# Second feed-forward of an encoder block: sums on VectorE, operands split one at a time, raw weights of the last matrix loaded from ScalarE's queue

## The chip, the cores and the metric

One core of a Trainium2 chip (trn2) runs the whole kernel. The core has a matrix engine (TensorE, PE in the profile), three engines for elementwise work (VectorE, DVE; ScalarE, ACT; GpSimd, POOL), an engine that mostly issues transfers (SyncE, SP), and 16 DMA engines that all queues share. An engine works through its own instructions in order; between engines, instructions wait on semaphores. The metric is device time in microseconds (us) for one execution.

## The reference

One layer of a streaming encoder over 1024 frames and 16 meta tokens, width 1024. The part that matters here is the last step, a SwiGLU feed-forward with 2816 hidden columns:

```python
def rmsnorm(x, g):
    xf = x.astype(jnp.float32)
    y = xf * lax.rsqrt(jnp.mean(xf * xf, axis=-1, keepdims=True) + EPS)
    return (y * g.astype(jnp.float32)).astype(x.dtype)

def swiglu(x, w_gate, w_up, w_down):
    return (jax.nn.silu(x @ w_gate) * (x @ w_up)) @ w_down
...
        h = h + mixed @ w_out[l]

        h = h + 0.5 * swiglu(rmsnorm(h, ffn2_norm[l]), ffn2_w_gate[l], ffn2_w_up[l], ffn2_w_down[l])
    return rmsnorm(h, final_norm)[:, N_META:]
```

Everything is fp32. Ahead of this come a first feed-forward, the attention, the gated linear attention and the merge; the change does not touch them.

## The kernel before

**Precision.** Each fp32 operand x is split in a rounded part hi (a cast on ACT) and a rest lo = x - hi (a subtraction on DVE); `halves` does both and puts hi and lo side by side in one tile. A product of two operands is three matmuls: hi*hi, hi*lo, lo*hi. A matmul is 128x128 weights against 512 columns.

**Seven products.** Data are transposed: 128 rows of features, 512 columns of tokens, so each feature tile has two token halves c = 0, 1. The two large matrices of the second feed-forward use a scheme with seven block products in place of eight (Strassen and Winograd), `PRODUCTS`: for the weights the blocks A11, A12, A22 and the sums S1 to S4, for the data B11, B21, B22 and T1 to T4. The products accumulate in three PSUM banks in the order b, a, b, d, b, d, b, and after a product the bank is read out, before a later product goes on adding to it. `Group.sums` makes S1 to S4 from two raw tiles, `Group.weights(i)` splits the weight operand of product i into a ring of eight tiles (wop), `Group.product` issues the matmuls. The scheduler runs the weights some seven products ahead, as far as the ring allows.

**Stages, in order of time.**

- w_out: for c = 0, 1 and m = 0 to 7 a product of 24 matmuls, the addition to h on DVE, a store to memory (h2_dram), and the sum of squares for the norm (acc). After each c, `scales_total` (a product with ones, tot, then the root, the reciprocal and a diagonal matrix dg) and `scales_spread` (a transpose, rep) turn acc into scales, and `rescale` and `halves` make the operands.
- Hidden tiles f = 0, 1 by ordinary products (`plain`), while T1 to T4 of the data are formed and split (tt).
- gate/up, `gate_up(f)`, f = 2 to 21: seven products of 12 matmuls, 84 in all. The raw tiles of gate and up come over SP's queue. ACT copies the bank after product 0 (L1172, g0), after product 2 (L1179, g1) and after product 3 (L1182, u1); DVE adds after products 1, 4, 5; ACT does the Silu; the two products of gate and up are on POOL (u1, L1189) and DVE. After two f, `middle` makes the seven data operands of the last matrix (B11, B21, T2, T1, T3, B22, T4); `keep` splits each (kh on ACT, kl on DVE) and stores both to memory (mid_dram).
- down: five groups (kg) of four hidden tiles, two halves each, 84 matmuls per half. Data operands (tm) are loaded from mid_dram, 512 KB each, raw weights in four loads of 256 KB per half, and h in tiles, all over SP's queue, in the order of the code. After each half product DVE adds half of the bank to h (L1252). There are two raw tiles, so a raw tile of the half after next waits until the last reader of the one in its place is done: casts, splits and POOL's sums.
- The last two hidden tiles by ordinary products, the final norm and the output.

## Time and profile before

| | |
|---|---|
| median of 3 runs | 2170.28 us (2168.26 to 2174.21) |
| the profiled execution | 2174.23 us |
| its span in the profile | 2172.5 us |
| mean granted TensorE clock | 0.987 |
| busy: TensorE, DVE, ACT, POOL | 2102.6, 1188.9, 707.8, 358.4 us |
| w_out between its column halves | 1387.4 to 1393.7 us |
| gate/up, f = 2 to 21 | 1484.55 to 1921.31 us |
| down | 1921.31 to 2129.26 us |

Times in the trace are from the start of the span. A row of a timeline has its start, its duration, the engine, the line, the operation, output and inputs, shapes, and in brackets the idle time just before it with what released it. Durations of matmuls overlap, since matmuls are pipelined: from start to start an undisturbed one takes less than its own duration. A row of waits has the waiting group, what it waited for, the total, how often, and the longest. A row of groups has the busy time and the mean of one in ns, then the idle time before them.

### The profile page before, as it was taken

The page shows a single profiled execution, that of the slowest core. Times are in us where ns is not written, and L with a number is a line of the kernel's source. Part 1 is how long each engine was busy: PE and PEld are TensorE (multiplying, and loading weights), DVE is VectorE, ACT ScalarE, POOL GpSimd, SP SyncE. Part 2 cuts the span into 40 slices and gives each one's busy share as a digit, 9 for nine tenths or more (in the row PEclk, how much of TensorE's full clock was granted, in tenths as well). Part 3 has the DMA queues.
Part 4 walks back from the last instruction along what each step waited for, and adds up shares of the span by engine and source line. Part 5 has one row for each costly group of instructions (what it writes and reads, how often), then busy time and mean ns, then how long its engine had stood idle before and what let it go on. Part 6 is the DMA issues. An engine that isn't in the chain of part 4 may idle for free.

```text
span 2172.5 us, 28898 instructions
## 1 busy us (share of the span) xinstructions
PE 2102.6 (97%) x11225; PEld 1866.1 (86%) x11225; DVE 1188.9 (55%) x1986; ACT 707.8 (33%) x1333; POOL 358.4 (16%) x320
## 2 busy tenths in 40 slices
PE   9999999999999999999999999998999999998998
PEld 8999999999999998888997788786777777786887
DVE  4644454444544446773534347458666556666776
ACT  6221111211112345663334233334443444322222
POOL 1000000000000260000100000124443435323322
PEclk9999999999999999999999999998999999999999
DMA  4211111111111221226112235533344334498732
GB/s 138 78 50 48 40 59 40 49 49 40 56 42 45 85 65 49 59 68 196 51 40 71 71 102 187 176 103 103 130 141 150 117 126 150 141 358 292 289 107 78
DMA packets 227641, 230.20 MB, mean 106 GB/s; under 512 B 19622, under 2 KB 174368, under 8 KB 227504
## 3 DMA queue, kind: packets, MB, share of 16 engines
q1 hardware_dynamic: 225840, 225.61, 32.1%
q10 hardware_dynamic: 1312, 2.63, 0.3%
q8 instruction: 88, 1.44, 0.3%
q14 instruction: 49, 0.40, 0.1%
q0 software_dynamic: 352, 0.11, 0.0%
HBM read 164.35 MB, written 63.96 MB: 105 GB/s over the span
## 4 chain that ended last, share of the span: by engine, by line
PE 85%; DVE 6%; DMA 4%; issue 2%; ACT 2%; POOL 1%; SPq 0%; DVEq 0%; POOLq 0%; ACTq 0%
PE pj L96 6%; PE pj L98 5%; PE pj L97 5%; PE pd L97 4%; PE pd L96 4%; PE pd L98 4%; PE pg L96 4%; PE pu L96 4%; PE pg L98 4%; PE pb L1112 4%; PE pg L97 4%; PE pu L98 4%; PE pu L97 4%; PE pb L1114 4%; PE pb L1113 4%
## 5 line engine op out<-in xcount | busy, mean ns | idle before, releaser
L204 ACT CAST whi<-raw 128x1024 fp32r<-128x1024 f32 x124 | 129.0, 1049 | 401.3 <-PE pd L97 189.8
L96 PE MATMUL pj<-u2h,whi 128*128 128x512 f32 (+2 forms) x608 | 228.8, 376 | 1.7 <-DVE o L902 1.7
L97 PE MATMUL pj<-u2l,whi 128*128 128x512 f32 (+2 forms) x608 | 223.7, 368 | 0.0
L98 PE MATMUL pj<-u2h,wlo 128*128 128x512 f32 (+2 forms) x608 | 223.7, 368 | 0.0
L96 PE MATMUL pg<-u1h,whi 128*128 128x384 f32 (+1 forms) x528 | 169.7, 321 | 2.0 <-ACT whi L204 2.0
L205 DVE TENSOR_TENSOR wlo<-raw,whi 128x1024 fp32r<-128x1024 f32 x121 | 149.1, 1239 | 40.2 <-ACT whi L204 35.2
L96 PE MATMUL pu<-u1h,whi 128*128 128x384 f32 (+1 forms) x528 | 169.6, 321 | 0.6 <-ACT u1q L181 0.6
L98 PE MATMUL pg<-u1h,wlo 128*128 128x384 f32 (+1 forms) x528 | 169.1, 320 | 0.6 <-DVE wlo L205 0.6
L97 PE MATMUL pg<-u1l,whi 128*128 128x384 f32 (+1 forms) x528 | 169.0, 320 | 0.0
L97 PE MATMUL pd<-ml,whi 128*128 128x384 f32 (+1 forms) x528 | 168.9, 320 | 0.0
L98 PE MATMUL pd<-mh,wlo 128*128 128x384 f32 (+1 forms) x528 | 168.5, 319 | 0.0
L96 PE MATMUL pd<-mh,whi 128*128 128x384 f32 (+1 forms) x528 | 168.5, 319 | 0.0
L98 PE MATMUL pu<-u1h,wlo 128*128 128x384 f32 (+1 forms) x528 | 168.4, 319 | 0.0
L97 PE MATMUL pu<-u1l,whi 128*128 128x384 f32 (+1 forms) x528 | 168.2, 319 | 0.0
L284 DVE SCALAR_TENSOR_TENSOR h<-pd,h 128x384 f32<-128x384 f32 (+1 forms) x240 | 122.8, 518 | 80.0 <-PE pd L98 79.3
L143 POOL TENSOR_TENSOR u2q<-u2q,sq 128x384 f32<-128x384 f32 (+1 forms) x21 | 19.6, 935 | 715.8 <-ACT sq L142 715.8
L1112 PE MATMUL pb<-tt,wop 128*128 128x512 f32 x240 | 99.3, 414 | 35.9 <-ACT g L1172 21.7
L96 PEld LDWEIGHTS pj<-u2h,whi 128*128 128x128 f32 x608 | 114.2, 188 | 20.6 <-issue 2.2
L98 PEld LDWEIGHTS pj<-u2h,wlo 128*128 128x128 f32 x608 | 114.1, 188 | 17.1
L1017 DVE TENSOR_TENSOR wop<-s,wop 128x512 fp32r<-128x512 f32 x120 | 93.6, 790 | 62.6 <-ACT wop L1016 62.2
L97 PEld LDWEIGHTS pj<-u2l,whi 128*128 128x128 f32 x608 | 114.3, 188 | 15.1
L1016 ACT CAST wop<-s 128x512 fp32r<-128x512 f32 x120 | 73.2, 623 | 136.3 <-POOL s L1095 65.5
(378 smaller groups left out, 4985.1 us busy)
## 6 DMA issues: line engine op xcount, KB each, us to landing
tm<-mid_dram SPq DMA_DIRECT2D x70, 512.0 KB, 8.9
raw<-in_ffn_w_gate SPq DMA_DIRECT2D x44, 512.0 KB, 4.0
raw<-in_ffn_w_up SPq DMA_DIRECT2D x44, 512.0 KB, 4.0
mid_dram<-kh SPq DMA_DIRECT2D x70, 256.0 KB, 2.3
mid_dram<-kl SPq DMA_DIRECT2D x70, 256.0 KB, 2.0
raw<-in_w_in SPq DMA_DIRECT2D x30, 512.0 KB, 3.9
raw<-in_ffn_w_down SPq DMA_DIRECT2D x24, 512.0 KB, 3.6
raw<-in_ffn_w_down SPq DMA_DIRECT2D x40, 256.0 KB, 4.8
```

The costliest lines, as they stand in the source:

```text
L96: nc.tensor.matmul(ps, wh[k], xh[k], start=(k == 0), stop=False)
L97: nc.tensor.matmul(ps, wh[k], xl[k], start=False, stop=False)
L98: nc.tensor.matmul(ps, wl[k], xh[k], start=False, stop=(k == n - 1))
L143: nc.gpsimd.tensor_add(a, a, sq[:, 0:n])
L204: nc.scalar.copy(hi[:, 0:cols], raw[:, 0:cols])
L205: (eng or nc.vector).tensor_sub(lo[:, 0:cols], raw[:, 0:cols], hi[:, 0:cols].bitcast(F32))
L284: nc.vector.scalar_tensor_tensor(hm, ps[:, 0:n], 0.5, hm, op0=ALU.mult, op1=ALU.add)
L1016: nc.scalar.copy(x[:, 0:HALF], src)
L1017: nc.vector.tensor_sub(x[:, HALF:], src, x[:, 0:HALF].bitcast(F32))
L1112: nc.tensor.matmul(ps, wh, xh, start=(first and k == 0), stop=False, skip_group_check=True)
L1113: nc.tensor.matmul(ps, wh, xl, start=False, stop=False, skip_group_check=True)
L1114: nc.tensor.matmul(ps, wl, xh, start=False, stop=(k == n - 1), skip_group_check=True)
```

## The change

Four things, in the order of the program:

1. The scales of the first column half of w_out and the rescaling and splitting of its eight tiles move from between the two column halves into the second one: the total behind product m = 0, the transpose behind m = 1, the tiles behind m = 1 to 7.
2. In gate/up the sums S1 to S4, the product for u1 and the differences of the pair move from POOL to DVE, and so do the differences for T1 to T4 ahead of it, where those of T4 are made only as T4 is split. `Group.sums` gets the engine as an argument; in down it stays POOL.
3. What `middle` makes of a pair goes to a list, `pending`, and `pump` takes one operand from it after each product of the following f: its difference, its split, its stores. After the last f the rest is emptied.
4. In down the raw weights are loaded over ACT's queue, issued ahead of product 6 of the half before. The loads of the data operands alternate with those of h, one operand at a time.

A small tile, shift2, is placed ahead of two of the ring's tiles; it only shifts an address.

```diff
@@ -1041,7 +1041,15 @@
             ps = bank("wo")
             cols = slice(c * HALF, (c + 1) * HALF)
             mm(ps, wh, wl, [t[:, cols] for t in mx_[0]], [t[:, cols] for t in mx_[1]])
+            if c == 1 and m == 0:
+                first_dg = scales_total(accs[0])
+            if c == 1 and m == 1:
+                scales_spread(accs[0], first_dg)
             nc.vector.tensor_add(hm, ps, hm)
+            if c == 1 and m >= 1:
+                for k in (range(2) if m == 1 else [m] if m < KT else []):
+                    rescale(k, 0)
+                    tops["B11" if k < 4 else "B21"][k % 4] = halves(operand(t_a, "tb"), ub[0][k])
             nc.sync.dma_start(out=h2_dram[c, m], in_=hm)
             if m == 0:
                 nc.scalar.activation(acc, hm, AF.Square)
@@ -1049,11 +1057,6 @@
                 sq = ttile("sq")
                 nc.scalar.activation(sq, hm, AF.Square)
                 (nc.vector if m >= KT - 2 else nc.gpsimd).tensor_add(acc, acc, sq)
-        if c == 0:
-            scales_spread(acc, scales_total(acc))
-            for m in range(KT):
-                rescale(m, 0)
-                tops["B11" if m < 4 else "B21"][m % 4] = halves(operand(t_a, "tb"), ub[0][m])
     acts.close()
 
     f2 = ctx.enter_context(ExitStack())
@@ -1061,6 +1064,8 @@
     shift = t_b.tile([P, 32], F32, name="shift", bufs=1)
     nc.gpsimd.memset(shift, 0.0)
     w_ext = f2.enter_context(tc.tile_pool(name="wext2", bufs=2))
+    shift2 = w_ext.tile([P, 32], F32, name="shift2", bufs=1)
+    nc.gpsimd.memset(shift2, 0.0)
     s_pool = f2.enter_context(tc.tile_pool(name="sums", bufs=4))
     ring, slot = [w_main] * 6 + [w_ext] * 2, [0]
 
@@ -1087,12 +1092,12 @@
             self.a = {"A11": a1[:, 0:HALF], "A12": a1[:, HALF:], "A21": a2[:, 0:HALF], "A22": a2[:, HALF:]}
             self.banks = {}
 
-        def sums(self):
+        def sums(self, eng):
             a = self.a
             for s, x, y, add in (("S1", "A21", "A22", True), ("S2", "S1", "A11", False),
                                  ("S3", "A11", "A21", False), ("S4", "A12", "S2", False)):
                 a[s] = s_pool.tile([P, HALF], F32, tag="s", name="s")
-                (nc.gpsimd.tensor_add if add else nc.gpsimd.tensor_sub)(a[s], a[x], a[y])
+                (eng.tensor_add if add else eng.tensor_sub)(a[s], a[x], a[y])
 
         def weights(self, i):
             w = ring_tile("wop")
@@ -1121,7 +1126,7 @@
     NAMES = [n for _, _, n in PRODUCTS]
     mid_dram = dram.tile([2 * NG, 7, P, 2 * HALF], F32, name="mid_dram")
     last_dram = dram.tile([LAST, 2, P, 2 * HALF], F32, name="last_dram")
-    pair = []
+    pair, pending = [], []
 
     def keep(dst, src):
         hi, lo = block("kh", F32R), block("kl", F32R)
@@ -1134,7 +1139,7 @@
 
         if f >= NF - LAST:
             for c, x in enumerate((m0, m1)):
-                keep(last_dram[f - (NF - LAST), c], x)
+                pending.append(lambda c=c, x=x: keep(last_dram[f - (NF - LAST), c], x))
             return
         pair.append((m0, m1))
         if f % 2 == 0:
@@ -1143,17 +1148,22 @@
         pair.clear()
         d = mid_dram[f // 2]
         t1, t2 = block("tm"), block("tm")
-        keep(d[NAMES.index("B11")], b11)
-        nc.vector.tensor_sub(t1, b12, b11)
-        nc.gpsimd.tensor_sub(b12, b22, b12)
-        keep(d[NAMES.index("B21")], b21)
-        nc.vector.tensor_sub(t2, b22, t1)
-        keep(d[NAMES.index("T2")], t2)
-        nc.gpsimd.tensor_sub(b21, b21, t2)
-        keep(d[NAMES.index("T1")], t1)
-        keep(d[NAMES.index("T3")], b12)
-        keep(d[NAMES.index("B22")], b22)
-        keep(d[NAMES.index("T4")], b21)
+
+        def work(n, src, sums=()):
+            def go():
+                for x in sums:
+                    nc.vector.tensor_sub(*x)
+                keep(d[NAMES.index(n)], src)
+            return go
+
+        pending.extend([
+            work("B11", b11, [(t1, b12, b11)]), work("B21", b21, [(b12, b22, b12)]),
+            work("T2", t2, [(t2, b22, t1)]), work("T1", t1, [(b21, b21, t2)]),
+            work("T3", b12), work("B22", b22), work("T4", b21)])
+
+    def pump():
+        if pending:
+            pending.pop(0)()
 
     def gate_up(f):
         raws = []
@@ -1170,24 +1180,31 @@
         b = product(0)
         g0 = block("g0")
         nc.scalar.copy(g0, b)
+        pump()
         a = product(1)
-        g.sums()
         nc.vector.tensor_add(g0, a, g0)
+        g.sums(nc.vector)
         nc.scalar.activation(g0, g0, AF.Silu)
+        pump()
         product(2)
         g1 = block("g1")
         nc.scalar.copy(g1, b)
+        pump()
         d = product(3)
         u1 = block("u1")
         nc.scalar.copy(u1, d)
+        pump()
         product(4)
         nc.vector.tensor_add(u1, b, u1)
+        pump()
         product(5)
         nc.vector.tensor_add(g1, d, g1)
         nc.scalar.activation(g1, g1, AF.Silu)
+        pump()
         product(6)
-        nc.gpsimd.tensor_mul(u1, u1, g1)
         nc.vector.tensor_mul(g0, b, g0)
+        nc.vector.tensor_mul(u1, u1, g1)
+        pump()
         middle(f, g0, u1)
 
 
@@ -1224,11 +1241,12 @@
     b11, b21, b12, b22 = ub[0][0:4], ub[0][4:8], ub[1][0:4], ub[1][4:8]
     for k in range(4):
         nc.vector.tensor_sub(b11[k], b12[k], b11[k])
-        nc.gpsimd.tensor_sub(b12[k], b22[k], b12[k])
+        nc.vector.tensor_sub(b12[k], b22[k], b12[k])
         nc.vector.tensor_sub(b22[k], b22[k], b11[k])
-        nc.gpsimd.tensor_sub(b21[k], b21[k], b22[k])
     for n, bs in (("T2", b22), ("T1", b11), ("T3", b12), ("T4", b21)):
         for k in range(4):
+            if n == "T4":
+                nc.vector.tensor_sub(b21[k], b21[k], b22[k])
             tops[n][k] = halves(operand(t_b, "tt"), bs[k])
             if n == "T2" and k == 1:
                 plain(0, 1)
@@ -1238,15 +1256,16 @@
         middle(f, *out_c[f])
     for f in range(2, NF):
         gate_up(f)
+    while pending:
+        pump()
 
 
     h2 = [[None] * 2 for _ in range(KT)]
 
-    def load_h(ms):
-        for r, c in ((0, 0), (0, 1), (4, 1), (4, 0)):
-            for m in ms:
-                h2[m + r][c] = block("h2")
-                nc.sync.dma_start(out=h2[m + r][c], in_=h2_dram[c, m + r])
+    def load_h(ms, r, c):
+        for m in ms:
+            h2[m + r][c] = block("h2")
+            nc.sync.dma_start(out=h2[m + r][c], in_=h2_dram[c, m + r])
 
     def add_half(hm, ps):
         nc.vector.scalar_tensor_tensor(hm, ps, 0.5, hm, op0=ALU.mult, op1=ALU.add)
@@ -1268,32 +1287,39 @@
             raw = raw_tile()
             wv = ffn2_w_down[kg * 4 * P:(kg + 1) * 4 * P, m * P:(m + 2) * P].rearrange("(a b p) m -> p b a m", b=2, p=P)
             for b in range(2):
-                nc.sync.dma_start(out=raw[:, b * HALF:(b + 1) * HALF].rearrange("p (a m) -> p a m", a=2), in_=wv[:, b])
+                nc.scalar.dma_start(out=raw[:, b * HALF:(b + 1) * HALF].rearrange("p (a m) -> p a m", a=2), in_=wv[:, b])
             raws.append(raw)
         return raws
 
     raws = load_weights(0, 0)
-    nxt = load_group(0, NAMES[0:3])
-    load_h((0, 1))
-    nxt.update(load_group(0, NAMES[3:]))
+    nxt = {}
+    where = ((0, 0), (0, 0), (0, 1), (4, 1), (4, 1), (0, 1), (4, 0))
+    for n, rc in zip(NAMES, ((0, 0), None, (0, 1), (4, 1), None, None, (4, 0))):
+        nxt.update(load_group(0, (n,)))
+        if rc:
+            load_h((0, 1), *rc)
     for kg in range(NG):
         ts = nxt
         for half in range(2):
             g = Group(*raws)
-            g.sums()
-            for i, (r, c) in enumerate(((0, 0), (0, 0), (0, 1), (4, 1), (4, 1), (0, 1), (4, 0))):
+            g.sums(nc.gpsimd)
+            for i, (r, c) in enumerate(where):
                 w = g.weights(i)
+                if i == 6:
+                    if half == 0:
+                        raws = load_weights(kg, 1)
+                    elif kg + 1 < NG:
+                        raws = load_weights(kg + 1, 0)
                 for j in range(2):
                     ps = g.product(i, w, ts, (j * P, 2 * P + j * P), j)
                     add_half(h2[2 * half + j + r][c], ps)
-            if half == 0:
-                raws = load_weights(kg, 1)
-                if kg == 0:
-                    load_h((2, 3))
-                if kg + 1 < NG:
-                    nxt = load_group(kg + 1, NAMES)
-            elif kg + 1 < NG:
-                raws = load_weights(kg + 1, 0)
+                if half == 0 and kg == 0 and i < 4:
+                    load_h((2, 3), *((0, 0), (0, 1), (4, 1), (4, 0))[i])
+                if kg + 1 < NG and (half == 0 or i < 7):
+                    if half == 0 and i == 0:
+                        nxt = {}
+                    if half == 0:
+                        nxt.update(load_group(kg + 1, (NAMES[i],)))
 
 
     mids = []
```

How this moves instructions. TensorE between the two column halves of w_out; tot and rep are the two steps of the scales of c = 0, wo the products (- before, + after, the @@ rows name positions):

```order
-L999 MATMUL tot<-ones,acc_11809 128x1 x4
-L1011 MATMUL rep<-ident,dg 128x128 x4
 L96 MATMUL wo<-mh_11425,whi 128x512
 L97 MATMUL wo<-ml_11433,whi 128x512
@@ -7720,4 +7718,5 @@
 L97 MATMUL wo<-ml_11440,whi 128x512
 L98 MATMUL wo<-mh_11432,wlo 128x512
+L999 MATMUL tot<-ones,acc_11809 128x1 x4
 L96 MATMUL wo<-mh_11425,whi 128x512
```

The total now follows one product of the second half, and the transpose (not shown) the next one.

ACT at the start of an f after a pair, before: kh are the casts of the pair's data operands, wop those of weights, and the copy of L1172 frees the bank of product 0.

```order
L1187 ACTIVATE g_13073<-g_13073 128x512
L1016 CAST wop<-raw 128x512
L1128 CAST kh<-g_13030 128x512
L1128 CAST kh<-tm 128x512
L1016 CAST wop<-raw 128x512
L1128 CAST kh<-tm 128x512
L1128 CAST kh<-u_12958 128x512
L1128 CAST kh<-u_13091 128x512
L1016 CAST wop<-s 128x512
L1128 CAST kh<-g_13030 128x512
L1172 COPY g_13211<-pb 128x512
```

And the same place after the change, where the copies after products 0, 2 and 3 are L1182, L1191 and L1195:

```order
L1202 ACTIVATE g_13075<-g_13075 128x512
L1016 CAST wop<-raw 128x512
L1182 COPY g_13167<-pb 128x512
L1016 CAST wop<-raw 128x512
L1133 CAST kh<-g_12853 128x512
L1133 CAST kh<-g_13032 128x512
L1016 CAST wop<-s 128x512
L1187 ACTIVATE g_13167<-g_13167 128x512
L1191 COPY g_13224<-pb 128x512
L1016 CAST wop<-s 128x512
L1133 CAST kh<-tm 128x512
L1195 COPY u_13249<-pd 128x512
```

All seven kh (six in this excerpt, one earlier) stood ahead of the first copy of the following f; now the first copy has none ahead, and they are spread over the products.

SP before, from the second half of h to the raw weights of the second group:

```order
L1249 DMA h_16196<-h_dram 128x512
L1260 DMA tm<-mid_dram 128x1024 x14
L1271 DMA raw<-in_ffn_w_down 128x2x256 x4
L1260 DMA tm<-mid_dram 128x1024 x3
L1271 DMA raw<-in_ffn_w_down 128x2x256 x2
```

and ACT after the change, from the last f into the first group of down:

```order
L1016 CAST wop<-raw 128x512
L1290 DMA raw<-in_ffn_w_down 128x2x256 x2
L1016 CAST wop<-s 128x512 x4
L1016 CAST wop<-raw 128x512
L1290 DMA raw<-in_ffn_w_down 128x2x256 x2
L1016 CAST wop<-raw 128x512 x2
L1290 DMA raw<-in_ffn_w_down 128x2x256
L1016 CAST wop<-s 128x512
L1290 DMA raw<-in_ffn_w_down 128x2x256
```

The raw loads have left SP's line behind the tm loads and stand among ACT's casts; one pair stands between the cast of A12 (the second wop<-raw) and the cast of S2 (the first wop<-s).

## The prediction

> **What bounds the kernel now.** I read the page's busy times first, then the waits of TensorE, then its timeline at the places that the waits name, then the other engines there. Of the engines (busy us, share of the span):
>
> ```profile
> PE 2102.6 (97%) x11225; PEld 1866.1 (86%) x11225; DVE 1188.9 (55%) x1986; ACT 707.8 (33%) x1333; POOL 358.4 (16%) x320
> ```
>
> TensorE is the bound, so only time in which it stands still or runs slowly can be won. Waits of TensorE from 1387 to 2130 us, which are all the stages that the change touches (total, times, longest):
>
> ```profile
> PE pb L1112 <- ACT g L1172: 21.7, 10, 9.6
> PE pb L1112 <- ACT g L1179: 14.3, 8, 1.8
> PE pb L1112 <- ACT wop L1016: 7.3, 2, 6.5
> PE pb L1112 <- DVE h L1252: 3.7, 1, 3.7
> PE tot L999 <- DVE acc L1051: 2.8, 1, 2.8
> PE rep L1011 <- DVE dg L1004: 1.0, 1, 1.0
> PE pb L1114 <- DVE wop L1017: 1.0, 1, 1.0
> ```
>
> These are 51.8 us. Waiting is not all: the clock falls after a wait, so I take the loss by counting. Timeline of TensorE (start, duration): a stretch of the down stage without a wait, and the first matmuls of gate/up, of down and of what follows.
>
> ```profile
> 1995.46 0.39 PE L1113 MATMUL pb<-tm,wop 128*128 128x512 f32 x1
> ...
> 2062.19 0.39 PE L1114 MATMUL pd<-tm,wop 128*128 128x512 f32 x1
> ```
>
> ```profile
> 1484.55 0.39 PE L1112 MATMUL pb<-tb,wop 128*128 128x512 f32 x1
> ...
> 1921.31 0.39 PE L1112 MATMUL pb<-tm,wop 128*128 128x512 f32 x1
> ...
> 2129.26 0.39 PE L96 MATMUL pd<-tl,whi 128*128 128x512 f32 x1
> ```
>
> 66.73 us between the first two over 293 matmuls is 0.2277 us each. Gate/up, f = 2 to 21, is 20 x 84 = 1680 matmuls, 382.5 us; it takes 436.8, so **54.2 us** are lost. Down is 5 groups x 2 halves x 84 = 840, 191.3 us; it takes 207.9, **16.7 lost**. The third place is w_out between its two column halves:
>
> ```profile
> 1387.35 0.39 PE L98 MATMUL wo<-mh,wlo 128*128 128x512 f32 x1
> 1390.55 1.32 PE L999 MATMUL tot<-ones,acc 128*128 128x1 f32 x8 [2.81 <-DVE acc L1051]
> 1392.90 1.11 PE L1011 MATMUL rep<-ident,dg 128*128 128x128 f32 x4 [1.03 <-DVE dg L1004]
> 1393.66 0.77 PE L96 MATMUL wo<-mh,whi 128*128 128x512 f32 x1
> 1394.24 0.63 PE L97 MATMUL wo<-ml,whi 128*128 128x512 f32 x1
> ```
>
> From 1387.58 to 1393.66 are 6.1 us, of which about 1.2 is tot's and rep's own work, which stays; the matmuls then start 0.43 apart for some ten, 1.9 us: **6.8 lost**. Together 77.7 us: the most that the change can win, 2174.2 - 77.7 = 2096.5 by the profiled execution.
>
> **The change part by part.** *w_out.* tot and rep now stand one product of 24 matmuls (5.5 us) behind what they wait for; the 2.81 and 1.03 lie under it. The eight rescaled tiles, two DVE instructions and one cast each, go under seven products of 5.5 us. Gain 6.8; I leave nothing.
>
> *Gate/up.* Why it waits: at 1504.74 TensorE comes back after 9.61 us on the copy of L1172, and ACT did this:
>
> ```profile
> 1497.54 0.62 ACT L1128 CAST kh<-m 128x512 fp32r<-128x512 f32 x1 [0.59 <-POOL m L1148]
> 1502.55 0.62 ACT L1016 CAST wop<-s 128x512 fp32r<-128x512 f32 x1 [4.39 <-POOL s L1095]
> 1503.08 1.13 ACT L1128 CAST kh<-m 128x512 fp32r<-128x512 f32 x2
> 1504.12 0.57 ACT L1172 COPY g<-pb 128x512 f32<-128x512 f32 x1
> ```
>
> The copy that frees the bank stands behind casts that wait for POOL. POOL and the subtractions on VectorE, f = 3 to 21:
>
> ```profile
> L1095 POOL TENSOR_TENSOR s<-raw,s 128x512 f32<-128x512 f32 x19 | 33.1, 1740 | 0.0
> L1189 POOL TENSOR_TENSOR u<-u,g 128x512 f32<-128x512 f32 x20 | 25.8, 1292 | 202.0 <-ACT g L1187 202.0
> L1129 DVE TENSOR_TENSOR kl<-u,kh 128x512 fp32r<-128x512 f32 x19 | 31.8, 1709 | 0.0
> L1186 DVE TENSOR_TENSOR g<-pd,g 128x512 f32<-128x512 f32 x20 | 13.8, 692 | 26.5 <-PE pd L1114 26.5
> 1511.00:1921.30 410.30, 383.98 (x1627) 309.65 (x1626) 249.49 (x297) 170.04 (x298) 171.30 (x114) 0.98 0.43 144
> ```
>
> (The last row is a window: length, then busy time and count of PE, PEld, DVE, ACT, POOL, then clock, DMA share, GB/s.) Per pair of f the change moves 8 sums, 2 products and 2 differences from POOL to DVE, which then has 14 split subtractions, 6 adds, 4 products, 8 sums, 4 differences and 7 kl: 43 instructions. At the 0.692 of L1186 they take 29.8 us; at DVE's mean of now, 249.49 / 297 = 0.84, they take 36.1. TensorE has 168 x 0.2277 = 38.3 us per pair, so the 12 added ones, 8.3 us a pair, are covered; uncovered they are 83 us over ten pairs. The 1709 comes from POOL's company on the same data, and POOL is now silent there. The stores of operands go out one per product, so one 0.62 us cast stands ahead of a copy, in place of two to four and POOL's 1.3 to 1.74. In the new order the g1 copy still stands behind the S2 cast and the Silu. S2 now hangs on the add after product 1: 5.46 us into f, plus three DVE instructions (2.1), cast (0.62), Silu (taken as long as a cast) and copy (0.57) is 9.4, and product 4 wants its bank at 48 x 0.2277 = 10.9. The margin is 1.5 us, where now it is negative. Sums on DVE need the raw tiles as POOL's did; a late one now stops DVE, and with it all reads of banks, where before it stopped POOL. That, and the last f (below), are why I leave 5 us of the 54.2 rather than nothing (bounds 0 and 20, that is 1 us in each f). The T operands ahead of f = 2 change hands in the same way (eight differences from POOL to DVE, 5.5 us at 0.69 under the 192 matmuls, 43.7 us, of the plain f = 0 and 1): the 1.03 on DVE's split goes or stays, and I count it with the 5.
>
> *Down.* The raw weights leave SP's queue, where they stood behind the operand loads (start, issuing time):
>
> ```profile
> 1941.48 13.85 SPq L1260 DMA_DIRECT2D tm<-mid_dram  x14
> 1956.31 4.14 SPq L1271 DMA_DIRECT2D raw<-in_ffn_w_down  x4
> ```
>
> ```profile
> 1966.72 0.80 PE L1112 MATMUL pb<-tm,wop 128*128 128x512 f32 x1 [6.53 <-ACT wop L1016]
> 1967.31 0.63 PE L1113 MATMUL pb<-tm,wop 128*128 128x512 f32 x1
> 1967.74 0.63 PE L1114 MATMUL pb<-tm,wop 128*128 128x512 f32 x1
> ```
>
> The raw loads go out at 1956.31, after 13.85 us of 14 loads of operands, and 10 us later TensorE comes back from its 6.53. The 3.70 comes 24 us later out of the same lateness. In the new order the raw loads are issued ahead of product 6 of the half before and nothing on ACT's queue stands ahead of them but casts: both waits go. The order of SP's own loads, one operand at a time between those of h, costs nothing as long as SP runs half a stage ahead; SP now shares semaphores with ACT's loads and can stand until a raw tile has landed, which only delays operands that TensorE wants a half (19.1 us) later. But ACT now waits where SP waited. The load of the next raw tile overwrites what POOL's S4 still reads; so ACT stands at the load until S4 is done, and behind it is the cast of S2, on which hangs the DVE's split of S2, ahead of product 2's adds, which free the bank of product 4. Now the cast waits for S2 alone. A half is 84 x 0.2277 = 19.1 us; three of them start at 2013.12 (its row below), 2032.25 and 2051.38, and POOL's sums in them are:
>
> ```profile
> 2021.27 1.76 POOL L1095 TENSOR_TENSOR s<-raw,s 128x512 f32<-128x512 f32 x1
> ...
> 2039.17 1.74 POOL L1095 TENSOR_TENSOR s<-raw,s 128x512 f32<-128x512 f32 x1
> ...
> 2058.24 1.29 POOL L1095 TENSOR_TENSOR s<-raw 128x512 f32<-128x512 f32 x1 [17.33 <-DMA raw<-in_ffn_w_down]
> ...
> 2062.10 1.73 POOL L1095 TENSOR_TENSOR s<-raw,s 128x512 f32<-128x512 f32 x1
> ```
>
> ```profile
> 2013.12 0.39 PE L1112 MATMUL pb<-tm,wop 128*128 128x512 f32 x1
> ...
> 2063.40 0.47 PE L1112 MATMUL pb<-tm,wop 128*128 128x512 f32 x1 [0.82 <-ACT wop L1016]
> ```
>
> S4 ends 9.9, 8.6 and 12.4 us into its half; cast (0.62), split and add (0.69 each, as L1186's) are 2.0 more; product 4 is due at 10.9. Late by 1.0, not, and 3.5 us. Seven halves repeat this: 0 to 24.5 us. I take 6, under their mean of 1.5, since the raw tiles no longer stand behind 512 KB loads, and the third is the one that landed late (it already costs the 0.82). At the entry the split of S2 for the second half stands ahead of the first adds; its raw tile is issued about 1 us before the entry, lands 4.8 later, S4 5.6 after that, and 2.0: 11.4 us in, where by the order TensorE needs the add after 40 matmuls, 9.1. With a landing as late as in the third half, 4 us more. I take 4 and 2 for the clock (0 to 9). The blocked ACT also holds the g1 copy in the last f: 1 us there is in gate/up's 5. Down keeps 12.
>
> ```profile
> raw<-in_ffn_w_down SPq DMA_DIRECT2D x40, 256.0 KB, 4.8
> ```
>
> The Trainium skill speaks against the moved loads: by its page "DMA: Bandwidth & Descriptors", section "Issuing engines are not separate DMA queues", all issuers share 16 engines, and another issuer saves issue time alone. Where that is all, down keeps its 16.7 and the sum would be 2118; the 13.85 us of issue ahead of the raw loads make me think that issue time is what they lack.
>
> After the 6.53 wait the matmuls start 0.43 apart (1967.31 to 1967.74), each 0.20 late; after the 0.82 wait the first is 0.47 long, not 0.63. So I price the clock at long waits alone. The Trainium skill ("TensorE: Matmul & The Clock Gate", Part 1) has the array at half clock after an idle window of about 3.4 us; the trace has it after less too, in w_out behind 2.81 us. Were each of seven late halves to carry 2 us of it, the sum would be 14 higher.
>
> **Sum.** 2174.2 - 77.7 + 5 + 12 = 2113.5 by the profiled execution. That one lies 3.9 over the median of the runs, 2170.3; the spread of the runs probably lies in the slow stretches, most of which go, so I take 1.5 off: **2112**.
>
> **Rivals.** *One, nothing comes back*: the raw tiles land as in the second half, every copy has its margin; some 2 us are left: 2098. For it speaks that two of three halves are late by 1 us or less. *Two, ACT behind S4 at full size*: each half as the third, 24.5, with the entry 9: 2174.2 - 77.7 + 5 + 33.5 = 2135. *Three, DVE's order takes the place of ACT's*: each instruction is in its place only once what stands ahead has run; if a bank is freed 2 us late in each f, gate/up keeps 40: 2174.2 - 77.7 + 40 + 12 = 2148. Against it is the 8 us of air per pair. *Four, slower*: DVE bounds gate/up. Ten pairs of 43 instructions then take 430 d; with w_out's and down's 11.5 won that is slower from d = (436.8 + 11.5) / 430 = 1.04 us on. At 1.1: 473 - 436.8 - 11.5 more, 2199. Rows of 1709 speak for it, their company with POOL against. *Five*, two and three at once, about 2170.
>
> **How the numbers follow.** Forecast 0.50, its own range 2101 to 2124; one 0.15, two 0.18, three 0.10, four 0.04, five 0.03. From 2096 to 2144 lie nearly all of the forecast, of one and two, and a third of three: 0.82. I call under 0.3% (6.5 us) no change: faster 0.93, same 0.03, slower 0.04.
>
> **What would show it.** Right: no POOL rows in gate/up; the waits for L1172 and L1179 (now L1182, L1191) near zero; DVE busy about 30 us in a window of 38.3; gate/up about 387 us; tot and rep without a wait. In down: a wait of 2 to 7 us some 9 us in, waits of about 1 us at product 4 released by ACT's cast, 203 us in all. Wrong: DVE at 1 us an instruction with POOL idle; waits of TensorE for DVE in each f; raw tiles that land 6 us into each half.

## The result, and the profile after

The changed kernel takes 2138.27 us (median of 4 runs, 2137.23 to 2140.25) beside 2172.24 for the kernel before (4 runs): ratio 0.9847, 95% interval 0.9829 to 0.9865. It is faster by 34 us, inside the range, but little more than half of the 58 that the forecast had (2170.28 to 2112): what came is rival two. The profiled execution's span is 2135.5 us, against 2172.5; it is the fastest of its four runs, and the profiled one of the kernel before is among its slowest, so the spans differ by 37.

The waits of TensorE from w_out to the end of down, in the changed kernel (group, what it waited for, total, times, longest):

```profile
PE pb L1117 <- DVE h L1271: 15.8, 5, 8.7
PE pb L1117 <- ACT wop L1016: 13.5, 3, 4.9
PE pb L1117 <- ACT g L1191: 1.4, 1, 1.4
```

Nothing is left in w_out, and in gate/up one wait of 1.4 us, in the last f. All the others lie in down, and there they are new. The timeline of TensorE has where the stages now begin:

```profile
1476.92 0.39 PE L1117 MATMUL pb<-tb,wop 128*128 128x512 f32 x1
...
1859.43 0.39 PE L1117 MATMUL pb<-tm,wop 128*128 128x512 f32 x1
...
2090.43 0.39 PE L96 MATMUL pd<-tl,whi 128*128 128x512 f32 x1
```

With the same rows of the kernel before this is the whole account:

| stage | before, us | after, us | difference |
|---|---|---|---|
| up to gate/up, f = 2 (w_out) | 1484.55 | 1476.92 | -7.6 |
| gate/up, 1680 matmuls | 436.8 | 382.5 | -54.3 |
| down, 840 matmuls | 207.9 | 231.0 | +23.1 |
| tail | 43.2 | 45.1 | +1.8 |
| span | 2172.5 | 2135.5 | -37.0 |

Gate/up runs at 382.5 / 1680 = 0.2277 us per matmul, the pace by which the prediction counted, and the 1.4 us wait is in it. Ahead of that wait, from 1476.92 to 1849.33, the 1643 steps from start to start take 0.2267 us each, so some 1.7 us are left to lose. Two windows of one pair's length there (length, then busy time and count of PE, PEld, DVE, ACT, POOL, then clock, DMA share, GB/s):

```profile
1477.00:1515.00 38.00, 38.00 (x169) 31.45 (x168) 29.70 (x48) 17.94 (x32) 0.00 (x0) 1.00 0.51 166
1515.00:1553.00 38.00, 38.00 (x169) 31.49 (x168) 27.51 (x43) 17.79 (x31) 0.00 (x0) 1.00 0.46 153
```

POOL has no row, and DVE does a pair's 43 instructions in 27.5 us, 0.64 each. Split subtractions that took 1.71 beside POOL take 0.74:

```profile
L1134 DVE TENSOR_TENSOR kl<-u,kh 128x512 fp32r<-128x512 f32 x19 | 14.1, 741 | 0.0
```

Down is where 23 us were given back. One half, timelines of five engines in the order of the chain; product 4 of this half is due at 1923.21 (the matmul ahead of the wait starts at 1922.98), so the half began 48 matmuls, 10.9 us, sooner, at 1912.3:

```profile
1911.19 0.91 ACTq L1290 DMA_DIRECT2D raw<-in_ffn_w_down  x2
```

```profile
1919.15 1.31 POOL L1100 TENSOR_TENSOR s<-raw 128x512 f32<-128x512 f32 x1 [17.72 <-DMA raw<-in_ffn_w_down]
1920.55 1.29 POOL L1100 TENSOR_TENSOR s<-s,raw 128x512 f32<-128x512 f32 x1
1921.80 1.30 POOL L1100 TENSOR_TENSOR s<-raw 128x512 f32<-128x512 f32 x1
1923.06 1.29 POOL L1100 TENSOR_TENSOR s<-raw,s 128x512 f32<-128x512 f32 x1
```

```profile
1924.39 0.90 ACTq L1290 DMA_DIRECT2D raw<-in_ffn_w_down  x2
1925.32 1.66 ACT L1016 CAST wop<-s 128x512 fp32r<-128x512 f32 x3 [9.46 <-POOL s L1100]
```

```profile
1926.05 0.69 DVE L1017 TENSOR_TENSOR wop<-s,wop 128x512 fp32r<-128x512 f32 x1 [7.39 <-ACT wop L1016]
1926.65 1.28 DVE L1271 SCALAR_TENSOR_TENSOR h<-pb,h 128x512 f32<-128x512 f32 x2
```

```profile
1927.44 0.76 PE L1117 MATMUL pb<-tm,wop 128*128 128x512 f32 x1 [4.07 <-ACT wop L1016]
1928.00 0.63 PE L1118 MATMUL pb<-tm,wop 128*128 128x512 f32 x1
```

S2 is ready at 1921.84, but ACT goes on to its cast only at 1925.32: it stands at the next raw load until S4 ends at 1924.35, and then issues two loads for 0.9 us. And POOL could begin only at 1919.15, 7 to 8 us after the loads were issued. From the issue to the moment that product 4 is due are 12.0 us. Landing 8.0, four sums 5.2, issue 0.9, and cast, split, add and their hand-overs 2.1 are 16.2; TensorE loses 4.2. In the kernel before the same chain was a landing of 4.8 in the median, two sums 2.6 and, from there to the matmul, 2.5 (S2 ends at 2060.9, TensorE is back at 2063.40): under 10. The half of these last figures is the one that landed late, with 8.0, and TensorE waited 0.82 there.

### The profile page after: what moved, and what is told of

The parts are those of the page before. It is cut to its first block, busy times and chain, and to the rows that moved or that the text cites. A ratio compares the mean times of both kernels' runs of the same rounds, so it can differ in the third digit from the quotient of the medians.

```text
span 2135.5 us, 28734 instructions
## 1 busy us (share of the span) xinstructions
PE 2085.5 (98%) x11225; PEld 1860.9 (87%) x11225; DVE 1195.6 (56%) x2114; ACT 707.3 (33%) x1333; POOL 158.2 (7%) x193
## 4 chain that ended last, share of the span: by engine, by line
PE 89%; DMA 4%; POOL 2%; DVE 2%; ACT 1%; issue 1%; ACTq 0%; POOLq 0%; DVEq 0%; SPq 0%
PE pj L96 6%; PE pj L97 6%; PE pj L98 6%; PE pu L96 4%; PE pg L96 4%; PE pg L98 4%; PE pg L97 4%; PE pu L98 4%; PE pu L97 4%; PE pb L1117 4%; PE pd L97 4%; PE pd L98 4%; PE pd L96 4%; PE pb L1118 4%; PE pb L1119 4%; DMA raw<-in_ffn_w_down 3%
## 5 line engine op out<-in xcount | busy, mean ns | idle before, releaser
L1017 DVE TENSOR_TENSOR wop<-s,wop 128x512 fp32r<-128x512 f32 x120 | 82.2, 688 | 86.3 <-ACT wop L1016 86.0
L96 PEld LDWEIGHTS pg<-u1h,whi 128*128 128x128 f32 x528 | 99.7, 189 | 2.1 <-ACT whi L204 1.9
L98 PEld LDWEIGHTS pg<-u1h,wlo 128*128 128x128 f32 x528 | 99.7, 189 | 1.0 <-DVE wlo L205 1.0
```

The costliest lines, as they stand in the source:

```text
L96: nc.tensor.matmul(ps, wh[k], xh[k], start=(k == 0), stop=False)
L98: nc.tensor.matmul(ps, wl[k], xh[k], start=False, stop=(k == n - 1))
L1017: nc.vector.tensor_sub(x[:, HALF:], src, x[:, 0:HALF].bitcast(F32))
```

## The experiments

Two theories. **One**: ACT stands at its raw load until S4 is done, ahead of S2's cast. **Two**: the raw tiles land late, since ACT's queue and SP's share the DMA engines, and the wait for S4 is incidental. Before that it had to be shown that the loss belongs to the down part, and not to TensorE's coming sooner.

**The down stage of before, in the changed kernel.** The block from the loads of h to the end of down is the old text:

```diff
-                nc.scalar.dma_start(out=raw[:, b * HALF:(b + 1) * HALF]...
+                nc.sync.dma_start(out=raw[:, b * HALF:(b + 1) * HALF]...
...
-    for n, rc in zip(NAMES, ((0, 0), None, (0, 1), (4, 1), None, None, (4, 0))):
-        nxt.update(load_group(0, (n,)))
+    nxt = load_group(0, NAMES[0:3])
+    load_h((0, 1))
+    nxt.update(load_group(0, NAMES[3:]))
...
```

> The changed kernel with the down stage of the kernel before: raw weights, data operands and h all on SP's queue again, in the old order; w_out and gate/up as changed. By the accounts of the two traces the changed down stage costs 23.1 us more than the old one (231.0 against 207.9) and the tail behind it 1.8, while the rest wins 61.9. If the stages add up, this runs in 2138 - 25 = 2113 us (ratio about 0.973), and its down stage takes about 208 us with its two old waits of some 6.5 and 3.7 us. If the gain of gate/up had only been passed on to down (the old down stage would meet the same lateness once TensorE comes sooner), it would be near 2138.

Measured: 2111.67 us, ratio 0.972 (0.9705 to 0.9734). Down takes 207.6 us (1858.20 to 2065.82). In down its waits are the two old ones and a small one:

```profile
1867.41 0.50 PE L1117 MATMUL pb<-tm,wop 128*128 128x512 f32 x1 [0.89 <-DVE h L1272]
1904.05 0.80 PE L1117 MATMUL pb<-tm,wop 128*128 128x512 f32 x1 [5.98 <-ACT wop L1016]
1928.27 0.80 PE L1117 MATMUL pb<-tm,wop 128*128 128x512 f32 x1 [3.48 <-DVE h L1272]
```

So the stages add up: the change without its down part is 27 us faster than with it.

**The changed down stage alone, in the kernel before.** The same block, the other way round.

> The kernel before with the changed down stage alone: raw weights on ACT's queue ahead of product 6, data operands one at a time between the loads of h; the rest as before. If the down part by itself is a loss, and the stages add up: 2172 + 25 = 2197 us, ratio 1.011, with waits of TensorE of 2 to 5 us in each half of down. If the loss comes from the faster gate/up ahead of it: no slower than before (ratio 1.00 or below).

Measured: 2198.90 us, ratio 1.0126 (1.0107 to 1.0145), slower by 27 us. By itself the down part is a loss of that size, behind the old gate/up as behind the new one. The waits at down's banks were expected at 2 to 5 us in each half; in the profile, which is of the slowest run, seven of the ten halves wait, by 0.3 to 8.4 us.

**A third raw tile.** In the changed kernel:

```diff
-    blk = right.enter_context(tc.tile_pool(name="blk", bufs=17, side="right"))
+    blk = right.enter_context(tc.tile_pool(name="blk", bufs=16, side="right"))
...
+    r_ext = f2.enter_context(tc.tile_pool(name="rext", bufs=1))
+    rring = [0]
...
-            raw = raw_tile()
+            rring[0] += 1
+            raw = raw_tile() if rring[0] % 3 else r_ext.tile([P, 1024], F32, tag="raw", name="raw")
```

> The changed kernel with a third raw tile in down (and 16 in place of 17 tiles for the hidden operands, to make room), so that a raw load on ACT's queue waits for readers half a stage ago and no longer for the S4 that POOL is just making. Theory one (ACT stands at the load until S4 is done, then issues two loads for 0.9 us, and only then casts S2): S2's cast comes 2.5 + 0.9 = 3.4 us sooner, so the waits at product 4 fall from 0.5 to 5.1 us to 0 to 1.7, their sum of 21.8 to about 5, with the slow clock behind them 25 us less in all: about 2113, ratio 0.973. Theory two (the raw tiles land late, since two queues share the DMA engines, and S2 itself is late): the landing is what it was, some 5 to 7 us into the half, and the waits shrink by under 1 us each: about 2133.

Measured: 2104.46 us, ratio 0.9687 (0.9672 to 0.9701), beyond what either theory had. Of all waits in down one is left:

```profile
1873.04 0.79 PE L1119 MATMUL pb<-tm,wop 128*128 128x512 f32 x1 [4.07 <-DVE h L1273]
```

But it does not tell the theories apart, as I had thought it would. A tile that comes free half a stage sooner takes away the wait for S4 and also lets the raw tiles be issued sooner (the last pair 53 us before the end of down, at 2004.48, in place of 39), so a late landing no longer matters. Two kernels that change one of these each had to follow.

**Sums of down on DVE.** In the changed kernel `g.sums(nc.gpsimd)` becomes `g.sums(nc.vector)`.

> The changed kernel with the four sums of down on DVE too (0.69 us each in place of 1.3 on POOL). ACT still waits for S4 at the raw load. Theory one: S4 is done 2.4 to 2.8 us after the landing in place of 5.2, and the adds that free the bank now stand ahead of S2's split in DVE's order; the waits at product 4 fall by 2.5 us or more each: 2110 to 2118, ratio about 0.974. Theory two: DVE, which works in order, stands at the late raw tile where POOL stood, and holds the adds: waits as now or longer, 2138 or more.

Measured: 2128.43 us, ratio 0.980 (0.9784 to 0.9817), 10 us faster than the change, less than half of what theory one had. The timeline of DVE has why:

```profile
1918.36 0.69 DVE L1100 TENSOR_TENSOR s<-raw 128x512 f32<-128x512 f32 x1 [7.36 <-DMA raw<-in_ffn_w_down]
1918.97 0.68 DVE L1271 SCALAR_TENSOR_TENSOR h<-pb,h 128x512 f32<-128x512 f32 x1
```

The sums are short now, but DVE stands 7.36 us at the raw tile that has not landed, with the adds behind it. Both theories had a part here.

**S4 off the raw tile.** The same instructions in the same places, other operands:

```diff
+            free = eng is nc.gpsimd
...
-                                 ("S3", "A11", "A21", False), ("S4", "A12", "S2", False)):
+                                 ("S3", "A22" if free else "A11", "A21", False),
+                                 ("S4", "S1" if free else "A12", "S2", False)):
```

> The changed kernel, but in down S3 is made as A22 - A21 and S4 as S1 - S2, so that POOL's S2 is the last sum that reads the raw tile that ACT overwrites; same instructions, same order, same loads at the same places (the values of S3 and S4, and with them the output, are not the reference's). ACT then waits for S2, which its next cast needs anyway, and not for S4, 2.5 us later. Theory one (the wait for S4): the seven waits at product 4 (3.6, 4.2, 2.1, 4.7, 0.5, 5.1, 1.6) and the one of the entry (8.9) lose up to 2.5 each: about 14 of 30.6 left, with some 5 us less of slow clock 2138 - 22 = 2116 to 2122. Theory two (the late landing alone): unchanged, 2138.

Measured: 2127.87 us, ratio 0.9798 (0.9783 to 0.9813): 10 us better than the change, where theory one had 16 to 22 and theory two none. In the timelines of POOL and ACT the wait for S4 is gone, S2 ends at 1918.47 and ACT goes on at once:

```profile
1915.84 1.30 POOL L1102 TENSOR_TENSOR s<-raw 128x512 f32<-128x512 f32 x1 [19.61 <-DMA raw<-in_ffn_w_down]
1917.21 1.26 POOL L1102 TENSOR_TENSOR s<-s,raw 128x512 f32<-128x512 f32 x1
```

```profile
1904.71 1.33 ACTq L1292 DMA_DIRECT2D raw<-in_ffn_w_down  x2
...
1918.51 0.90 ACTq L1292 DMA_DIRECT2D raw<-in_ffn_w_down  x2
```

But the loads issued at 1904.71 let POOL begin only at 1915.84, 11 us later, and TensorE still waits 5.27 us in this half. The edit did not leave the landings as they were. From the issue of a raw pair to POOL's S1, and by how much product 4 of that half is late (from start to start, which is some 0.15 more than the idle time in the row), in the order of the halves:

| half behind the entry | 1 | 2 | 3 | 4 | 5 | 6 | 7 |
|---|---|---|---|---|---|---|---|
| change: issue to S1, us | 6.4 | 8.0 | 5.7 | 8.3 | 3.8 | 8.9 | 5.1 |
| change: late | 3.6 | 4.2 | 2.1 | 4.7 | 0.5 | 5.1 | 1.6 |
| S4 off: issue to S1, us | 5.7 | 11.1 | 5.6 | 11.1 | 3.6 | 9.7 | 5.1 |
| S4 off: late | 1.6 | 5.4 | 0 | 5.4 | 0 | 4.1 | 0 |

The long waits are those of the late landings. In halves 2, 4 and 6 the landing came 3.1, 2.8 and 0.8 us later without the wait for S4, and product 4 is 1.2 and 0.7 later and 1.0 sooner: some 2 us less than the landings alone would add. Halves 3, 5 and 7 landed nearly as before and lose their waits; the entry falls from 8.9 to 6.0. So at an equal landing the wait for S4 costs some 2 us where there are 2 to win, and the 10 us are what the later landings left of that. Why they came later no run shows.

**No operand loads after the first group.** In the changed kernel:

```diff
-                    if half == 0 and i == 0:
-                        nxt = {}
-                    if half == 0:
-                        nxt.update(load_group(kg + 1, (NAMES[i],)))
+                    nxt = ts
```

> The changed kernel without the loads of data operands after the first group: all five groups use the operands of the first (56 loads of 512 KB are left out, and the output is not the reference's). ACT still waits for S4. What is measured is how late the raw tiles land because of the other queue. Without that traffic I expect a raw tile some 3.5 us after its issue in place of 5.5 to 8, at 3 to 4 us into the half; then S4 5.2, two issues 0.9, cast, split and add 2.0: 11.1 to 12.1 against the 10.9 at which product 4 is due. Both theories have shorter waits here; theory one, 0.2 to 1.2 us each, in all about 2138 - 22 = 2116 (the entry stays); if the engines' load is no part of it: 2138.

Measured: 2114.98 us, ratio 0.9742 (0.9725 to 0.9759), 23 us better than the change and near the 2116 expected. ACT still waits for S4, and yet after the first two waits (9.9 and 4.2 us) there is none over 0.6. The median from issue to landing (KB each, us), in down after the change and here:

```profile
raw<-in_ffn_w_down ACTq DMA_DIRECT2D x33, 256.0 KB, 5.5
```

```profile
raw<-in_ffn_w_down ACTq DMA_DIRECT2D x34, 256.0 KB, 3.0
```

So neither theory alone is right. Of the 27 us that the down part costs, taking away the wait for S4 gave back 10, although three landings came later with it, and taking away the traffic of the operand loads gave back 23 with the wait for S4 left as it is. They stand in one chain with 12 us to spend, so shortening either part helps until the chain fits, and the gains do not add. The 5.5 and 3.0 us run from the issue on, and ACT issues a raw load as soon as its tile is free (at 1924.39, where S4 ends at 1924.35), so it is the transfers that the traffic slows, and not a wait ahead of them. A wait of that kind is SP's: by the inferred releasers its operand loads stand until raw tiles have landed (changed kernel, 1855 to 2060 us, waits of SP's queue: total, times, longest).

```profile
SPq L1279 <- DMA raw<-in_ffn_w_down: 60.9, 11, 9.0
```

**Raw loads back on SP, in the new place.** `nc.scalar.dma_start` becomes `nc.sync.dma_start`, nothing else.

> The changed kernel with the raw weights of down issued from SP at the same place of the program (ahead of product 6), all else as changed. ACT is free of loads and of S4. Theory one: the waits of 0.5 to 5 us at product 4 go, except where the raw tile itself lands late; but at the entry the raw tile of the second half now stands behind the loads of operands and h, as it did before the change, so one wait of some 6 us and one of some 3.5 come back: about 2112. Theory two: raw tiles behind 512 KB loads land later still: 2140 or more.

Measured: 2126.51 us, ratio 0.9793 (0.9777 to 0.981), 12 us better than the change, but 15 worse than the old down stage. The waits in each half are gone (one of 4.47 is left), but one at the entry is far longer than I had:

```profile
1898.07 0.79 PE L1117 MATMUL pb<-tm,wop 128*128 128x512 f32 x1 [19.05 <-ACT wop L1016]
```

Its cause is on SP's queue, where the raw tiles of the second half now stand behind all the loads of h and of operands:

```profile
1862.37 3.47 SPq L1268 DMA_DIRECT2D h<-h_dram  x6
...
1888.23 3.56 SPq L1290 DMA_DIRECT2D raw<-in_ffn_w_down  x4
```

26 us lie between those rows. So ACT's queue does help at the entry, as the prediction had it (6.5 and 3.7 in the old order, 19 here, 8.7 and 3.4 with ACT's queue), and costs in the halves behind it.

**Third raw tile, and h loaded first.** The first two tiles of h are loaded ahead of the last hidden tiles' split and store:

```diff
-    while pending:
-        pump()
...
+    load_h((0, 1), 0, 0)
+    while pending:
+        pump()
```

> The kernel with the third raw tile (2104 us), with the first two tiles of h loaded ahead of the last hidden tiles' split and store, so that the first adds of down no longer wait for h. In the third-tile kernel the only wait left in down is 4.1 us there, with a slow clock behind it that I put at 2 us. Expected 2098, ratio 0.966. If h is only the last of several late things there (S2's split stands right ahead of it in DVE's order, 3.8 us sooner), 2103.

Measured: 2101.90 us, ratio 0.9679 (0.9664 to 0.9694). The wait at the entry falls from 4.07 to 3.10 us and is no longer for h; the interval overlaps that of the third tile alone (0.9672 to 0.9701), so this is at most a small gain, nearer to the 2103 that was expected if h is only the last of several late things. With 196.6 us down is 5 above its 191.3. It beats both kernels: 36 us faster than the change.

**Gate/up, one edit at a time.** Two edits went together there. First POOL has its work back and only the spreading stays:

```diff
-        g.sums(nc.vector)
+        g.sums(nc.gpsimd)
...
+        nc.gpsimd.tensor_mul(u1, u1, g1)
-        nc.vector.tensor_mul(u1, u1, g1)
...
-                    nc.vector.tensor_sub(*x)
+                    (nc.gpsimd if n in ("B21", "T1") else nc.vector).tensor_sub(*x)
```

> The changed kernel with gate/up's sums, the product for u1 and two differences of the pair back on POOL, as before; only the spreading of the operands over the products, w_out and down stay changed. It tells which of the two edits won gate/up's 54 us. If the jam of casts ahead of the copies was the cause, the spreading alone wins most: gate/up some 385 to 395 us (382.5 with both, 436.8 before), 2141 to 2151 in all. If POOL's 1.3 to 1.7 us sums, late after the raw tile, and their company on DVE's data were the cause: 420 us and more, 2175.

Measured: 2144.05 us, ratio 0.9871 (0.9846 to 0.9896); gate/up takes 391.8 us (1478.70 to 1870.45). Second, DVE has the work, but the operands are split and stored in one lump:

```diff
             work("T3", b12), work("B22", b22), work("T4", b21)])
+        while pending:
+            pump()
...
```

> The changed kernel with all operands of a pair split and stored at once at the end of the pair, as before, but with the sums, the product and the differences on DVE. If the jam of casts was the cause, gate/up keeps most of its loss: seven casts at 0.53 are 3.7 us of ACT ahead of or between the copies, and DVE has 11 instructions, 7.6 us, in one lump ahead of the adds, 2 us or more at each of 10 pairs with a slow clock behind: 405 to 435 us, 2160 to 2190 in all. If POOL was the cause: 383 to 390 us, 2139 to 2146.

Measured: 2146.17 us, ratio 0.9879 (0.9854 to 0.9903); gate/up takes 388.5 us (1479.39 to 1867.92). From the 436.8 of before each edit alone wins 45 to 48 of the 54 us. The jam needs both: a lump of casts ahead of the copies, and POOL's share of the work. That POOL acts by the late inputs of the casts is what the rows in the prediction suggest; its company also slows DVE's subtractions, and these kernels do not separate the two. What I expected of the lump on DVE, that casts alone would hold most of the loss, was wrong: TensorE's only waits in gate/up are 2.1 and 0.5 us there.

## Why the prediction was right or wrong

**The count of the loss: right.** The loss was there to be won by the count of matmuls (77.7 us) and not by the sum of waits (51.8): the best kernel here gains 70. The 66.73 us are 292 steps from start to start and not 293, 0.2285 each, so the count is some 2 us too high. w_out and gate/up gave 61.9 where the count had 61.0.

**w_out and gate/up: right, better than forecast.** tot and rep have no wait. DVE at 0.64 us an instruction stays under TensorE, as the 0.692 of L1186 said. That row reads a bank, though, and such rows take 0.69 beside POOL too (last section), so it alone could not show what the others would do with POOL idle: that the figure held for them was partly luck. The old mean of 0.84 was POOL's company, and rivals three and four, which needed a late or a slow DVE, did not come. The 5 us that I left were not needed. The 1.4 us in the last f are the held copy of g1 that I put at 1. Which of the two edits does it I had not asked; the answer is either.

Some 3 us of the 54 belong to neither of the two. In the kernel before, three of every eight products, as many as the ring has tiles, take 2.76 to 2.80 us from start to start, without a wait; the others take 2.72:

```profile
2006.16 0.39 PE L1112 MATMUL pb<-tm,wop 128*128 128x512 f32 x1
...
2008.92 0.40 PE L1112 MATMUL pd<-tm,wop 128*128 128x512 f32 x1
...
2011.72 0.39 PE L1112 MATMUL pb<-tm,wop 128*128 128x512 f32 x1
...
2014.49 0.39 PE L1112 MATMUL pb<-tm,wop 128*128 128x512 f32 x1
...
2017.21 0.39 PE L1112 MATMUL pa<-tm,wop 128*128 128x512 f32 x1
```

In the changed kernel all that neither wait nor follow a wait take 2.72. The excess is 0.17 us in eight products, 3.0 in the 140 of gate/up and 1.5 in the 70 of down. Both kernels without shift2, the one before and the one with the changed down stage alone, have this pattern, and none with shift2 has it. So the address that this tile shifts is the likely cause; no run has the tile alone, and it is not shown.

**Down: the right mechanism, mis-sized.** The prediction has each place: the waits at product 4 behind S4, the wait at the entry, and what releases them. The terms were too small (measured from start to start, as in the table by halves):

| term | predicted | measured |
|---|---|---|
| seven halves | 6 | 21.8 (3.6, 4.2, 2.1, 4.7, 0.5, 5.1, 1.6) |
| entry, wait | 4 | 8.9 |
| slow clock behind them | 2 | 9.0 (39.7 less the waits) |
| down above 191.3 | 12 | 39.7 |

The step that failed is "I take 6, under their mean of 1.5, since the raw tiles no longer stand behind 512 KB loads". They no longer stand behind them in a queue, but they run at the same time: in down the 256 KB loads take 5.5 us after the change and 5.0 before (4.8 in the whole kernel). I took the half with the late landing, 3.5 us, for the exception. It was issued at 2050.23 and POOL began 8.0 us later:

```profile
2050.23 1.19 SPq L1271 DMA_DIRECT2D raw<-in_ffn_w_down  x2
```

In the changed kernel three of seven halves are like it or later (8.0, 8.3, 8.9), and in four of seven S1 begins more than 6 us into its half, which I had named as a sign of being wrong. The rule of the Trainium skill that I had weighed and set aside ("DMA: Bandwidth & Descriptors", "Issuing engines are not separate DMA queues": loads of several issuers run on the same engines and interleave) agrees with this: without the operand loads the same raw loads take 3.0. Its other half, that only issue time is saved, gave 2118 in the prediction, nearer to 2138 than my 2112. It has no loss in it either, and there is one: with SP as issuer in the same place the kernel is 12 us faster.

A second omission is the cost of issuing on ACT. Two loads take 0.9 us of ACT between S4 and the cast (1924.39 above), which is no term of my sum: up to 6 us over seven halves.

At the entry the landing was 4.8 in the sum. The second half's raw tile is issued at 1859.20, its two loads land 7.9 and 9.5 us after their issue, and POOL begins at 1869.28, 10 us later, in the burst of loads there (the releaser in the row is inferred; by the order S1 needs this raw tile):

```profile
1859.20 1.06 ACTq L1290 DMA_DIRECT2D raw<-in_ffn_w_down  x2
```

```profile
1869.28 1.26 POOL L1100 TENSOR_TENSOR s<-raw 128x512 f32<-128x512 f32 x1 [20.27 <-DMA last_dram<-kl]
```

I had "4 us more" only as the upper bound.

**The clock.** Of the waits in the changed kernel those of 4.1 us and more are followed by matmuls 0.43 apart (1928.00 to 1928.43 is one such step), the ones of 3.41 and 1.9 are not. That I priced the clock at long waits alone was right; the waits were longer than I thought. The Trainium skill's idle window of about 3.4 us ("TensorE: Matmul & The Clock Gate", Part 1) fits these rows, but the runs do not show it as a threshold. In the kernel with the lump on DVE the matmuls are 0.43 apart behind a wait of 2.88 us too (1961.82 to 1962.24), and in the changed kernel not behind 3.41. The 2.81 of w_out, which the prediction set against the window, is the weaker case, since a second wait of 1.03 us follows it ahead of the slow matmuls.

**The old waits in down: gone, as said.** No wait of 6.5 or 3.7 at their old places; the price of it was paid in each half.

**Rival two** had 2135, with all of these terms at their upper bounds and 5 us left in gate/up. Its mechanism came, but that its time fits within 3 us is in part luck: its 33.5 for down is 6 below the 39.7, since it priced no slow clock behind the seven halves, and the 5 in gate/up, which did not come, make up for most of it. The 1.8 us that the tail took more have no explanation here. The chance of 0.18 was too low.

## What to carry to other kernels

Before a load is moved to an engine's own queue, write down the whole chain from the load's issue to the first matmul that needs it, with the load's own waits in it and what stands behind it on that engine; a chain that fits in the time (10 of 12 us here with the median landing) may not after the move (13.7 with the median landing of 5.5, 16.2 with one of 8). A load that must wait for the reader of the tile that it overwrites belongs on a queue with nothing urgent behind it, or gets one more tile: here that one tile took 34 us off the change. And a jam of two causes may need only one of them removed, so try each edit alone.

## What the runs showed of the hardware that was not expected

A split subtraction on DVE took 1.71 us while POOL worked beside it, and 0.74 for the same shape and operands with POOL idle; I had expected it to fall, but not that DVE's pace as a whole would reach 0.64 per instruction. Between 1490 and 1850 us the kernel before has DVE instructions on 128x512 with both inputs outside the banks at 0.69 us wherever no POOL row overlaps them and at up to 1.79 beside one; those that read a bank take 0.69 in both cases. How long a 256 KB raw load takes from its issue depends on what the other queue moves: 3.0 us in the median without the operand loads on SP's queue and 5.5 with them, and single pairs 8 to 11.
